# A convolution block: the product steps of a streamed job in one run, row chunks and convolution tile behind them

## The chip, the core and the metric

The kernel runs on one core of a Trainium2 chip. The metric is the device time of one execution in microseconds. The kernel before takes 1061.26 us, the median of 3 runs (1061.01 to 1061.35).

TensorE (PE in the rows) multiplies; VectorE (DVE), ScalarE (ACT) and GpSimdE (POOL) do the rest; SyncE (SP) issues most transfers from memory. Each engine takes its instructions in the order in which they stand in its own queue, and waits at one whose inputs or buffer aren't ready.

## The reference

One layer of a decoder, 256 tokens by 2048 features, in float32. `c` is a condition vector:

```python
mod = silu(c) @ mod_w + mod_b                      # 2048 -> 12288
sh1, sc1, g1, sh2, sc2, g2 = split(mod, 6)
h = rms_norm(x, norm1_g) * (1 + sc1) + sh1
a, gt = split(h @ w_in + b_in, 2)                  # 2048 -> 4096
u = a * sigmoid(gt)
u = depthwise_causal_conv(u, dw_w, 31 taps) + dw_b
y = silu(layer_norm(u, ln_g, ln_b)) @ w_out + b_out
x = x + (1 + g1) * y
h = rms_norm(x, norm2_g) * (1 + sc2) + sh2
x = x + (1 + g2) * (square(relu(h @ w1)) @ w2)     # 2048 -> 8192 -> 2048
```

## The kernel before, in words

Activations lie with features on the 128 partitions and tokens along the row. float32 products run as three products of rounded high parts and remainders: ScalarE writes the high part of a weight half (`hi`, line 245), GpSimdE subtracts it and writes the remainder (`lo`, line 252), and in `mm` two matmuls a step, `hi` by the pair of activations (line 276) and `lo` by the high activations (line 277), give all three.

The product with `w_in` makes 32 column tiles of 128. They go in pairs, one of `a` and one of `gt`: a pair is a job, ("in", 0) to ("in", 15). The first eight jobs share one pass while the input is normalised. The jobs 8 to 15 are streamed: each takes two weight tiles of 1 MB, and its 32 steps (16 for each of the two tiles) are 64 matmuls. Jobs 8 to 14 end in `evac` and `gate`: ScalarE copies one half of the sums (line 953), VectorE adds the other (line 954), ScalarE takes the sigmoid (line 1232) and VectorE multiplies (line 1234, "gate" below). The sums lie in one of two `mm` tiles of PSUM, and these two alternate with the convolution tiles, so that the job after next, or the next one where a convolution lies between, waits for the gate.

Between the jobs other work is handed out by tables. `LATE_IN` gives jobs 8 to 14 row chunks of the modulation matrix, 4, 4, 4, 4, 3, 4 and 1: a chunk is a 1 MB load and four matmuls 32 columns wide that run beside each other (`mod_chunk`, line 737). `CONV_AT` gives the jobs 9, 10, 11, 12, 14 and 15 a convolution tile for TensorE (`pe_conv`, line 1215, 32 matmuls); ScalarE first makes 16 shifted copies (`copy_wide`, line 1189) and afterwards takes the sum out (line 1225). Eight other tiles go over VectorE, tap by tap (lines 1070 to 1076, `advance`). Tile 9 is made by ScalarE's products (line 1129) and GpSimdE's additions (line 1132). `find_shift` (line 1139) sums the first two convolution tiles on TensorE (line 834) and ScalarE makes two copies of the mean (line 1145), which the first taps of the later tiles need (line 1074). After the second group of sixteen chunks a row is copied out (line 744) and folded by four small matmuls (line 781).

Weights and chunks share a ring of five 1 MB buffers (`raw`, line 200). SyncE issues the loads in one fixed order, and a load waits until the buffer's last reader is done: GpSimdE's second `lo` for a weight tile, the four matmuls for a chunk.

A scheduler places the instructions on their engines by its own estimate of when each can run, and `tc.issue_after(x)` says only that an instruction stands behind x. So the queues' order, and not the order of the source, is what the chip sees.

Of the kernel before, what the change touches and what calls it, by code (L numbers as in the profile page):

```python
# [17 lines left out]
KT = D // P  # L18
# [69 lines left out]
def conv_block(ctx: ExitStack, tc: tile.TileContext, x, vec, dwq, c_row, mod_r, mod_c, w_first, w_in, w_out, w1, w2, out):  # L88
# [44 lines left out]
    for i in range(2):  # L133
        p = ps.tile([P, 2, 2 * T], F32, name="mm", bufs=2)
# [6 lines left out]
    state = {"used": 0}  # L141
# [16 lines left out]
    HALF = KT // 2  # L158
# [105 lines left out]
    def mm(p, c, key, acts_of, ks=range(KT), merged=False):  # L264
        halves = parts[key]
        for k in ks:
            hi, lo = halves[k // HALF]
            m = acts_of[k // 2][:, k % 2, :]
            if merged:
                out_p, begin, end = p[:, c, 0:T], k == 0, k == KT - 1  # L270
                w = hi[:, k % HALF, :]
                nc.tensor.matmul(out_p, w, m[:, 0:T], start=begin, stop=False)  # L272
                nc.tensor.matmul(out_p, w, m[:, T : 2 * T], start=False, stop=False)  # L273
                state["mm_end"] = nc.tensor.matmul(out_p, lo[:, k % HALF, :], m[:, 0:T], start=False, stop=end)  # L274
                continue
            nc.tensor.matmul(p[:, c, :], hi[:, k % HALF, :], m, start=(k == 0), stop=(k == KT - 1))  # L276
            state["mm_end"] = nc.tensor.matmul(  # L277
                p[:, c, T : 2 * T], lo[:, k % HALF, :], m[:, 0:T], start=False, stop=(k == KT - 1),
                skip_group_check=True,
            )  # L280
# [446 lines left out]
    def mod_chunk(nb, kg):  # L727
        w = take(("mod", nb, kg))
        group = next(g for g in GROUPS if nb in g)
        b = group.index(nb)  # L730
        begin, end = b == 0 and kg == 0, b == len(group) - 1 and kg == 3
        if begin:
            mod_finish()
            row_ps.append(ps.tile([P, 512], F32, name="row", bufs=1))
        for k in range(4):
            part = w[k // 2][:, 4 * (k % 2) : 4 * (k % 2) + 4, :] if isinstance(w, list) else w[:, 4 * k : 4 * k + 4, :]
            state["row_end"] = nc.tensor.matmul(  # L737
                row_ps[0][32 * k : 32 * k + 32, :], cz[:, 4 * kg + k, 3 - b : 35 - b], part,
                start=begin, stop=end,
            )  # L740
        if end:
            r = tmp.tile([P, 512], F32, name="rowsb", bufs=1)
            with urgent(), tc.issue_after(state["hi_end"]):
                nc.scalar.activation(r, row_ps.pop(), AF.Copy)
            pending.append(([4 * nb for nb in group], 4, r))
# [57 lines left out]
    def mod_col(at):  # L803
        w = take(("col", at)).rearrange("p k n -> p (k n)")
        which, k = divmod(at, KT)
        acc = modc[:, at : at + 1]
        if which == SH2 and "cond" in state:
            n = HALF * P
            for half, total in zip(state["cond"], (acc, rest2[:, k : k + 1])):
                nc.vector.scalar_tensor_tensor(w[:, 0:n], w[:, 0:n], 1.0, half, op0=ALU.mult, op1=ALU.mult, accum_out=total)  # L810
                w = w[:, n:]
            return
        with tc.issue_after(state["e_end"]) if "e_end" in state else ExitStack():
            nc.vector.scalar_tensor_tensor(w, w, 1.0, cb, op0=ALU.mult, op1=ALU.mult, accum_out=acc)  # L814
        if which in amps:
            return nc.vector.scalar_tensor_tensor(
                amps[which][:, k : k + 1], acc, col("modb", at), col("n1g", k), op0=ALU.add, op1=ALU.mult
            )
        elif which != SH2:
            return mod_bias(at, 1, acc)  # L820

    def mods(keys):
        for key in keys:
            if key[0] == "mod":
                mod_chunk(*key[1:])
            else:
                mod_col(key[1])
# [46 lines left out]
    hl = [None] * HALF  # L874
# [86 lines left out]
    p = ps.tile([P, 512], F32, name="small", bufs=1)  # L961
# [10 lines left out]
    with urgent():  # L972
        part = two()[:, 0, :]
        nc.scalar.activation(part, p[:, 0:T], AF.Copy)
        p = ps.tile([P, 512], F32, name="row", bufs=1)
# [8 lines left out]
    for _ in range(2):  # L984
        p = ps.tile([P, 2, 2 * T], F32, name="mm", bufs=2)
# [36 lines left out]
    for k in range(KT):  # L1022
        c = k % 2
# [85 lines left out]
    def advance(n):  # L1109
        for _ in range(n):  # L1110
            next(conv_taps, None)
# [27 lines left out]
    def find_shift():  # L1139
        state["small"] = ps.tile([P, 512], F32, name="small", bufs=1)  # L1140
        p = state["small"][:, 0:T]
        column_sum(p, [cv(k) for k in range(SHIFT)])
        state["shift"] = cp.tile([P, T], F32, name="shift", bufs=1)
        for dst in (state["small"][:, T : 2 * T], state["shift"]):
            nc.scalar.activation(dst, p, AF.Copy, scale=-1.0 / (SHIFT * P))
# [58 lines left out]
    def pe_conv(ct, sq=None, between=None):  # L1204
        wide = wides.pop(ct)
        diag = diags.pop(ct)
        p = ps.tile([P, 2, 2 * T], F32, name="mm", bufs=2)[:, 0, 0:T] if sq is None else ps_two()[:, 0, :]
        if sq is not None:
            nc.tensor.matmul(p, col("ident", 0, P), state["shift"], start=True, stop=False)
        for m in range(8):  # L1210
            if between is not None and m == LAST_TAPS:
                between()
            for g in range(4):
                with tc.issue_after(state["stats_end"].ins) if between is not None else ExitStack():
                    state["conv_end"] = nc.tensor.matmul(  # L1215
                        p[32 * g : 32 * g + 32, :], diag[:, 8 * g + m, :], wide[:, g, 4 * m : 4 * m + T],
                        start=(m == 0 and sq is None), stop=(m == 7),
                    )
        with urgent():
            if ct == 14:  # L1220
                state["cv14"] = nc.vector.scalar_tensor_tensor(
                    cv(ct), p, col("dwb", ct), state["shift"], op0=ALU.add, op1=ALU.add
                ).ins
            elif sq is None:
                nc.scalar.activation(cv(ct), p, AF.Identity, bias=col("dwb", ct))
            else:
                state["cv15"] = nc.vector.tensor_scalar(cv(ct), p, col("dwb", ct), None, op0=ALU.add).ins
                nc.scalar.activation(sq, p, AF.Square, bias=col("dwb", ct))
# [10 lines left out]
    def mix(ct):  # L1239
        pe_conv(ct)  # L1240
        if ct == SHIFT - 1:
            find_shift()
# [16 lines left out]
    for n, job in enumerate(jobs):  # L1259
# [15 lines left out]
        kind, i = job[0], job[-1]  # L1275
        if kind == "out" and i > 0:
            p = ps_two()
        elif not by_tokens(job):
            p = ps.tile([P, 2, 2 * T], F32, name="mm", bufs=2)
# [3 lines left out]
        if job == ("up", 0, 0):  # L1283
            first = mm_shifted(p, 0, job + (0,), False)
            for _ in range(SIDE):
                next(first)
            shift_row(shown.pop(job + (0,)))
            fold_shift()
            for _ in chain(first, mm_shifted(p, 1, job + (1,))):
                pass  # L1290
        elif plain:
            for _ in chain(*[mm_shifted(p, c, job + (c,)) for c in range(2)]):
                pass
        elif job in K_OUTER:
            for k2 in range(HALF):
                for c in range(2):
                    mm(p, c, job + (c,), hl, range(2 * k2, 2 * k2 + 2), True)
        elif kind == "in":
            rows = list(after[job]) if i < KT - 1 else []
            if i == KT - 1:  # L1300
                state["e_end"] = state["copied"]
                mods(cols_in[:COLS_FIRST])
            for c in range(2) if i < KT - 1 else (1, 0):
                for ks in (range(HALF), range(HALF, KT)):
                    mm(p, c, job + (c,), hl, ks, i == KT - 1)
                    with tc.issue_after(state["mm_end"].ins):
                        mods(rows[:1])
                    del rows[:1]
            if i == KT - 1:
                room["hl"] = len(rows_in_hl)  # L1310
                top_up()
        elif by_tokens(job):
            mm_tokens(sums, job)
            state["mm_end"] = state["three_end"]
        else:
            for c in range(2):
                mm(p, c, job + (c,), hl, merged=kind == "out")
        mod_finish()
        if kind == "in":
# [12 lines left out]
            for ct in CONV_AT.get(n, ()):  # L1332
                with tc.issue_after(state["mm_end"].ins):
                    mix(ct)
            advance(ADVANCE.get(n, 0))
            if n in PAIRS_AT:
                pool_pairs(PAIRS_AT[n])
# [34 lines left out]
            rows = after[job][COLS_IN:]  # L1372
# [238 lines left out]
```

## Time and profile before

| | us |
|---|---|
| median of 3 runs | 1061.26 |
| span of the profiled execution, first to last instruction | 1059.2 |
| what lies around the span, median less span | 2.1 |
| first matmul of job 8, in the span | 137.04 |
| first matmul of job 15 | 264.26 |
| TensorE busy | 1042.9 |
| VectorE busy | 918.1 |
| ScalarE busy | 678.2 |
| GpSimdE busy | 280.3 |

All instants below are microseconds from the start of the span. The profile gives the profiled execution's span and no other time of it. A float32 matmul shows as two records, a step's matmuls as one each; records overlap, so the distance from one start to the next tells what a matmul costs, not its own duration.

### The profile page before, as it was taken

The numbers are of one execution on the slowest core, as the hardware profiler recorded it, in microseconds if no ns is written. First come the engines' busy times: TensorE is split into PE (matmuls) and PEld (weight loads), VectorE is DVE, ScalarE is ACT, GpSimd is POOL, SyncE is SP. The second block draws the span as 40 slices with busy tenths as digits, with TensorE's granted clock in tenths as the row PEclk, the third lists the DMA queues.
The fourth block names the chain that finished last, engine by engine and source line by source line (L and its number), as shares of the span: only waits on it lengthen the run. The fifth ranks groups of instructions, "written<-read, shape, count | busy, mean of one in ns | idle before, by whom it ended". The sixth has DMA issues, their size and how long they took to land.

```text
span 1059.2 us, 15571 instructions
## 1 busy us (share of the span) xinstructions
PE 1042.9 (98%) x5712; PEld 853.6 (81%) x5712; DVE 918.1 (87%) x1200; ACT 678.2 (64%) x969; POOL 280.3 (26%) x267
## 2 busy tenths in 40 slices
PE   6999999999999999999999999999999999999998
PEld 3888876676789999877888888888888888888887
DVE  5778779998785889999989999999999999999975
ACT  4111198765776579674777587587687686696771
POOL 0000076979359721001210210111110200113130
PEclk8999999999999999999999999999999999999999
DMA  9999989898989999759998999998999898997892
GB/s 382 420 420 416 411 349 366 308 362 355 368 359 326 357 390 323 215 189 334 332 295 300 279 317 293 274 337 269 279 333 279 280 330 272 282 325 235 308 292 100
DMA packets 75662, 335.20 MB, mean 316 GB/s; under 512 B 9249, under 2 KB 9761, under 8 KB 57409
## 3 DMA queue, kind: packets, MB, share of 16 engines
q1 hardware_dynamic: 57456, 279.53, 70.4%
q0 software_dynamic: 13664, 46.68, 18.1%
q10 hardware_dynamic: 4466, 8.00, 2.0%
q8 instruction: 45, 0.74, 0.3%
q14 instruction: 31, 0.25, 0.1%
HBM read 322.10 MB, written 12.07 MB: 315 GB/s over the span
## 4 chain that ended last, share of the span: by engine, by line
PE 83%; DMA 10%; DVE 4%; ACT 2%; issue 1%; SPq 0%; DVEq 0%; ACTq 0%
PE mm L309 14%; PE mm L308 14%; PE mm L310 14%; DMA raw<-mod_c 7%; PE mm L276 4%; PE acc L309 4%; PE acc L310 4%; PE acc L308 4%; PE acc L272 3%; PE acc L274 3%; PE acc L273 3%; DVE raw L814 2%; PE mm L277 2%; PE row L737 2%; PE mm L1215 1%; PE row L309 1%
## 5 line engine op out<-in xcount | busy, mean ns | idle before, releaser
L324 DVE TENSOR_TENSOR lo<-raw,hi 128x1024 fp32r<-128x1024 f32 x238 | 283.2, 1217 | 30.2 <-ACT hi L327 29.7
L327 ACT ACTIVATE hi<-raw 128x1024 fp32r<-128x1024 f32 x238 | 241.8, 1052 | 71.3 <-DVE raw L324 30.2
L308 PE MATMUL mm<-hi,u 128*128 128x512 f32 x448 | 174.9, 390 | 0.0
L309 PE MATMUL mm<-lo,u 128*128 128x512 f32 x448 | 174.9, 390 | 0.0
L310 PE MATMUL mm<-hi,u 128*128 128x512 f32 x448 | 174.5, 390 | 0.0
L252 POOL TENSOR_TENSOR lo<-raw,hi 128x1024 fp32r<-128x1024 f32 x52 | 124.0, 2410 | 160.5 <-ACT hi L245 160.5
L327 ACT ACTIVATE hi<-s 128x1024 fp32r<-128x1024 f32 x80 | 83.3, 1056 | 101.4 <-DVE s L324 88.9
L814 DVE SCALAR_TENSOR_TENSOR raw<-raw,cond 128x2048 f32<-128x2048 f32 x47 | 109.0, 2323 | 19.4 <-DMA raw<-mod_c 19.4
L324 DVE TENSOR_TENSOR lo<-s,hi 128x1024 fp32r<-128x1024 f32 x80 | 97.5, 1221 | 3.9 <-ACT hi L327 2.3
L309 PEld LDWEIGHTS mm<-lo,u 128*128 128x128 f32 x448 | 84.1, 188 | 18.7 <-DVE lo L324 1.5
L308 PEld LDWEIGHTS mm<-hi,u 128*128 128x128 f32 x448 | 84.2, 188 | 17.8 <-issue 0.2
L310 PEld LDWEIGHTS mm<-hi,u 128*128 128x128 f32 x448 | 84.2, 188 | 17.2
L1076 DVE SCALAR_TENSOR_TENSOR acc<-u,v,acc 128x256 f32<-128x256 f32 x224 | 94.5, 483 | 1.8
L245 ACT ACTIVATE hi<-raw 128x1024 fp32r<-128x1024 f32 x80 | 80.3, 1048 | 11.5 <-DMA raw<-w_in 4.1
L475 POOL DMA_DIRECT2D s<-w x28 | 15.5, 552 | 269.4 <-DVE lo L324 206.6
L276 PE MATMUL mm<-hl,hi 128*128 128x512 f32 x224 | 81.7, 406 | 0.5 <-DVE u L1234 0.5
L1039 ACT ACTIVATE two<-two,modc,amp 128x256 f32<-128x256 f32 x16 | 9.6, 600 | 95.4 <-DVE modc L772 67.6
L999 PE MATMUL mm<-two,first 128*128 128x256 f32 x256 | 60.7, 392 | 7.4 <-ACT two L1039 6.7
L272 PE MATMUL acc<-hl,hi 128*128 128x256 f32 x224 | 63.4, 283 | 0.0
L273 PE MATMUL acc<-hl,hi 128*128 128x256 f32 x224 | 63.4, 283 | 0.0
L277 PE MATMUL mm<-hl,lo 128*128 128x256 f32 x224 | 63.4, 283 | 0.0
L274 PE MATMUL acc<-hl,lo 128*128 128x256 f32 x224 | 63.3, 283 | 0.0
(287 smaller groups left out, 2355.9 us busy)
## 6 DMA issues: line engine op xcount, KB each, us to landing
raw<-w SPq DMA_DIRECT2D x212, 512.0 KB, 6.9
raw<-mod_c SPq DMA_DIRECT2D x56, 1024.0 KB, 11.4
s<-w POOLq DMA_DIRECT2D x68, 512.0 KB, 8.5
raw<-mod_r SPq DMA_DIRECT2D x26, 1024.0 KB, 8.0
raw<-w_in SPq DMA_DIRECT2D x16, 1024.0 KB, 7.0
raw<-w_out SPq DMA_DIRECT2D x16, 1024.0 KB, 9.7
first<-w_first SPq DMA_DIRECT2D x15, 1024.0 KB, 17.2
raw<-mod_c SPq DMA_DIRECT2D x16, 512.0 KB, 12.6
```

The costliest lines, as they stand in the source:

```text
L252: end = by.tensor_tensor(lo, w[:, ks, :], hi.bitcast(F32), op=ALU.subtract)
L272: nc.tensor.matmul(out_p, w, m[:, 0:T], start=begin, stop=False)
L273: nc.tensor.matmul(out_p, w, m[:, T : 2 * T], start=False, stop=False)
L274: state["mm_end"] = nc.tensor.matmul(out_p, lo[:, k % HALF, :], m[:, 0:T], start=False, stop=end)
L276: nc.tensor.matmul(p[:, c, :], hi[:, k % HALF, :], m, start=(k == 0), stop=(k == KT - 1))
L308: nc.tensor.matmul(p, x_hi, w_hi, start=begin, stop=False, skip_group_check=not grouped)
L309: nc.tensor.matmul(p, x_hi, w_lo, start=False, stop=False, skip_group_check=not grouped)
L310: state["three_end"] = nc.tensor.matmul(p, x_lo, w_hi, start=False, stop=end, skip_group_check=not grouped)
L324: ordered("dve", lambda: call(*args, **kw))
L327: ordered("act", lambda: nc.scalar.activation(*args, **kw))
L814: nc.vector.scalar_tensor_tensor(w, w, 1.0, cb, op0=ALU.mult, op1=ALU.mult, accum_out=acc)
L1076: nc.vector.scalar_tensor_tensor(out, s, w, acc, op0=ALU.mult, op1=ALU.add)
```

## The change

The 64 matmuls of a streamed job stand in one run. All row chunks of the job come behind them, then its convolution tile, and the next job's steps behind the last of these.

```diff
-                for ks in (range(HALF), range(HALF, KT)):
-                    mm(p, c, job + (c,), hl, ks, i == KT - 1)
-                    with tc.issue_after(state["mm_end"].ins):
-                        mods(rows[:1])
-                    del rows[:1]
+                with tc.issue_after(state["behind"].ins) if "behind" in state else ExitStack():
+                    mm(p, c, job + (c,), hl, merged=i == KT - 1)
+            with tc.issue_after(state["mm_end"].ins):
+                mods(rows)
+            if rows:
+                state["behind"] = state["row_end"]
...
             for ct in CONV_AT.get(n, ()):
                 with tc.issue_after(state["mm_end"].ins):
                     mix(ct)
+                state["behind"] = state["conv_end"]
```

On TensorE, where job 9 begins, before (`mm_845` holds the sums of job 8, `mm_1017` those of job 9; the `raw` tiles are chunks):

```order
L277 MATMUL mm_845<-hl_653,lo_770 128x256
L276 MATMUL mm_1017<-hl_208,hi_810 128x512
L737 MATMUL row_864<-raw_678,cz_720 32x512 x4
L277 MATMUL mm_1017<-hl_208,lo_811 128x256
L276 MATMUL mm_1017<-hl_208,hi_810 128x512
```

And the same place now:

```order
L277 MATMUL mm_845<-hl_653,lo_770 128x256
L737 MATMUL row_912<-raw_678,cz_720 32x512 x4
L737 MATMUL row_912<-raw_684,cz_720 32x512 x4
L737 MATMUL row_912<-raw_735,cz_720 32x512 x4
L737 MATMUL row_912<-raw_763,cz_720 32x512 x4
L276 MATMUL mm_1017<-hl_208,hi_810 128x512
```

The four chunks of job 8 stood spread over job 9's steps; now all four stand ahead of them.

On TensorE, where the first group's row is folded, before (`mm_1674` is job 12):

```order
L277 MATMUL mm_1674<-hl_388,lo_1437 128x256
L276 MATMUL mm_1674<-hl_450,hi_1440 128x512
L781 MATMUL row_1552<-v_72,rowsb_1550 128x4 x4
L277 MATMUL mm_1674<-hl_450,lo_1441 128x256
L276 MATMUL mm_1674<-hl_450,hi_1440 128x512
```

Now the end of job 11 (`mm_1461`), its chunks, its convolution tile (`mm_1567`) and job 12:

```order
L277 MATMUL mm_1461<-hl_653,lo_1216 128x256
L737 MATMUL row_912<-raw_1301,cz_720 32x512 x4
L737 MATMUL row_912<-raw_1307,cz_720 32x512 x4
L737 MATMUL row_912<-raw_1313,cz_720 32x512 x4
L1215 MATMUL mm_1567<-wide_1219,diag_1422 32x256 x4
L737 MATMUL row_912<-raw_1319,cz_720 32x512 x4
L1215 MATMUL mm_1567<-wide_1219,diag_1422 32x256 x20
L781 MATMUL row_1552<-v_72,rowsb_1550 128x4 x4
L1215 MATMUL mm_1567<-wide_1219,diag_1422 32x256 x8
L276 MATMUL mm_1674<-hl_208,hi_1426 128x512
```

The fold stood three quarters into job 12's steps; now it stands ahead of all of them.

On ScalarE, around the mean that the later taps need (`mm_1331` is the convolution tile behind job 10, `sq` are products for tile 9, `hi` halves of weights), before:

```order
L1129 ACTIVATE sq_1408<-u0_81,v2_79 128x256 x4
L1225 ACTIVATE cv0_716<-mm_1331,v_72 128x256
L1189 ACTIVATE wide_1444<-u1_82 32x284 x16
L1145 ACTIVATE small_1365<-small_1365 128x256
L1129 ACTIVATE sq_1415<-u0_81,v2_79 128x256 x4
L1145 ACTIVATE shift_1368<-small_1365 128x256
L245 ACTIVATE hi_1426<-raw_1199 128x1024
```

And now:

```order
L1129 ACTIVATE sq_1408<-u0_81,v2_79 128x256 x4
L245 ACTIVATE hi_1426<-raw_1199 128x1024
L245 ACTIVATE hi_1430<-raw_1199 128x1024
L1129 ACTIVATE sq_1415<-u0_81,v2_79 128x256 x4
L1225 ACTIVATE cv0_716<-mm_1331,v_72 128x256
L1189 ACTIVATE wide_1444<-u1_82 32x284 x16
L245 ACTIVATE hi_1436<-raw_1209 128x1024
L1145 ACTIVATE small_1365<-small_1365 128x256
L245 ACTIVATE hi_1440<-raw_1209 128x1024
L1145 ACTIVATE shift_1368<-small_1365 128x256
L953 ACTIVATE two_1561<-mm_1461 128x512
```

Two weight halves and the second set of products moved ahead of the convolution's copy, and two more halves ahead of the mean's copies.

## Rows read from the trace of the kernel before

**Rows 1.** The page, busy time of each engine and its share of the span.

```profile
PE 1042.9 (98%) x5712; PEld 853.6 (81%) x5712; DVE 918.1 (87%) x1200; ACT 678.2 (64%) x969; POOL 280.3 (26%) x267
```

**Rows 2.** Timeline of TensorE, job 8: start, duration, line, operation, records, idle before.

```profile
137.04 0.58 PE L276 MATMUL mm<-hl,hi 128*128 128x512 f32 x1
...
148.32 0.39 PE L276 MATMUL mm<-hl,hi 128*128 128x512 f32 x1
148.64 1.07 PE L737 MATMUL row<-raw,cz 128*32 128x512 f32 x8
...
149.86 0.39 PE L276 MATMUL mm<-hl,hi 128*128 128x512 f32 x1
```

**Rows 3.** Timeline of TensorE, chunks in a run, behind job 15.

```profile
290.63 3.62 PE L737 MATMUL row<-hl,cz 128*32 128x512 f32 x32
294.07 1.04 PE L737 MATMUL row<-raw,cz 128*32 128x512 f32 x8
```

**Rows 4.** Line 226 in the stretch of the fourth chunk's load: issue, time to landing.

```profile
L226 SPq DMA_DIRECT2D raw<-mod_r x1: 328/328/328, 149.8 to 149.8; - x1
...
DMA to landing us min/median/max: 5.1/5.1/5.1
```

**Rows 5.** Timeline of VectorE, gates, taps and sums.

```profile
160.39 0.49 DVE L1234 SCALAR_TENSOR_TENSOR u<-mm,v,two 128x256 f32<-128x256 f32 x1 [1.00 <-ACT two L1232]
...
172.34 12.62 DVE L1076 SCALAR_TENSOR_TENSOR acc<-u,v,acc 128x256 f32<-128x256 f32 x32
185.19 0.70 DVE L954 TENSOR_TENSOR mm<-mm,two 128x512 f32<-128x512 f32 x1 [0.24 <-ACT two L953]
...
186.98 0.48 DVE L1234 SCALAR_TENSOR_TENSOR u<-mm,v,two 128x256 f32<-128x256 f32 x1
...
198.88 0.88 DVE L1074 SCALAR_TENSOR_TENSOR acc<-u,v,small 128x256 f32<-128x256 f32 x2 [0.86 <-ACT shift L1145]
```

**Rows 6.** Timeline of ScalarE, halves, sums, sigmoids, copies and products.

```profile
180.11 3.89 ACT L245 ACTIVATE hi<-raw 128x1024 fp32r<-128x1024 f32 x4
...
185.93 0.47 ACT L1232 ACTIVATE two<-mm,v 128x256 f32<-128x256 f32 x1 [0.77 <-DVE mm L954]
...
189.04 0.47 ACT L1225 ACTIVATE cv<-mm,v 128x256 f32<-128x256 f32 x1 [1.05 <-PE mm L1215]
189.41 7.17 ACT L1189 ACTIVATE wide<-u 32x284 f32<-32x284 f32 x16
196.50 0.36 ACT L1145 ACTIVATE small<-small 128x256 f32<-128x256 f32 x1
196.88 1.71 ACT L1129 ACTIVATE sq<-u,v 128x256 f32<-128x256 f32 x4
...
218.03 0.58 ACT L744 ACTIVATE rowsb<-row 128x512 f32<-128x512 f32 x1
```

**Rows 7.** Timeline of GpSimdE, remainders of two weight tiles, a diagonal, sums of products.

```profile
182.18 9.44 POOL L252 TENSOR_TENSOR lo<-raw,hi 128x1024 fp32r<-128x1024 f32 x4
191.57 1.92 POOL L1197 TENSOR_TENSOR diag<-v,dwq_sb 128x1024 f32<-128x1024 f32 x1
193.45 2.65 POOL L1132 TENSOR_TENSOR pairs<-pairs,sq 128x512 f32<-128x512 f32 x2
```

**Rows 8.** Timeline of TensorE, the fold, and from job 14's convolution to job 15.

```profile
221.27 0.95 PE L781 MATMUL row<-v,rowsb 128*128 128x4 f32 x8
...
259.42 3.64 PE L1215 MATMUL mm<-wide,diag 128*32 128x256 f32 x64
262.87 0.39 PE L1155 MATMUL small<-cv,ones 128*32 128x256 f32 x2
...
264.26 0.39 PE L272 MATMUL mm<-hl,hi 128*128 128x256 f32 x1
```

**Rows 9.** Busy time by stretch near the start: stretch, length, engines, TensorE's granted clock.

```profile
20.00:25.00 5.00, 4.72 (x12) 3.81 (x13) 4.66 (x7) 0.88 (x3) 0.00 (x0) 0.53 1.01 421
```

**Rows 10.** Timeline of TensorE, two sets of 16 first products.

```profile
20.28 5.88 PE L999 MATMUL mm<-two,first 128*128 128x256 f32 x16 [4.64 <-ACT two L1039]
...
93.86 3.72 PE L999 MATMUL mm<-two,first 128*128 128x256 f32 x16 [0.88 <-ACT two L1039]
```

## The prediction

> **What bounds the kernel now.** I read the busy shares first: TensorE is busy for 98% of the span, VectorE for 87%, ScalarE for 64%, GpSimdE for 26% [rows 1]. What delays TensorE is therefore paid, unless it idles later anyway; what delays another engine is paid only where TensorE ends up waiting for it. Next I read the streamed stretch on TensorE's timeline. Job 8 begins at 137.04 and job 15 at 264.26, so 127.2 us hold jobs 8 to 14 with 24 chunks and five convolution tiles. Job 8's 64 matmuls take from 137.04 to 148.32, 11.3 us, .176 each and .353 a pair [rows 2]. TensorE hardly waits in this stretch; the releasers that come closest are VectorE's gate, which is followed by the next use of the same PSUM tile, and ScalarE's copies [rows 5, 6].
>
> **The switch that the change removes.** A chunk's four matmuls are 32 columns wide, a step's 128. From one step to the next across one chunk it takes 149.86 − 148.32 = 1.54 us; without the pair itself, .353, the chunk costs 1.19 [rows 2]. In a run of chunks four of them take 294.07 − 290.63 = 3.44, .86 each [rows 3]. So going over to narrow matmuls and back costs .33 for each place, not for each chunk. Of the 24 chunks 16 stand alone among steps now; the other 8 already stand beside a convolution tile, which is narrow too. Afterwards only jobs 8 and 13 have a block of chunks without a convolution tile, so two new places are paid: 14 × .33 = 4.6 us saved. If nothing else moved, job 15 would begin at 259.6.
>
> **The chunk that isn't there yet.** The ring has five buffers, and job 8's fourth chunk goes into that of its first. Before, that load was issued at 149.8, right behind the first chunk, and landed 5.1 later, 154.9, in time for its place three quarters into job 9 [rows 4]. Now it is still issued about 149.8 (the first chunk ends there), but TensorE reaches the fourth chunk at 148.64 + 3 × .86 = 151.2. It waits 154.9 − 151.2 = 3.7 us, and all of job 9 stands behind it. That alone eats four fifths of the saving. It need not reach the end, because VectorE has a later date for job 10 in any case:
>
> **VectorE's order.** In the new order 31 taps and 2 joins stand between job 8's gate and job 9's sum; before there were 16 taps. A tap takes 12.62 / 32 = .39 [rows 5], and I price a join like one. Gate 8 ends near 160.9 (160.39 + .49); 33 × .39 = 12.9 puts job 9's sum at 173.8; from sum to end of gate it is 187.46 − 185.19 = 2.27 in the rows of another job [rows 5], so gate 9 ends at 176.0. Job 10 needs its PSUM tile. TensorE itself, with the 3.7 us, would come at about 174.9 (154.9 + .86 for the chunk, 11.3 for job 9, 3.44 for its chunks, 3.45 for its convolution tile and three switches). So from here the date is VectorE's, whether the chunk was late or not; job 10 runs 176.0 to 187.3, and with four chunks (3.44), a convolution (3.45, below) and two switches job 11 begins near 195.
>
> **ScalarE's order, first place.** The convolution's sum behind job 10 has to be copied out before `find_shift` can use it, a quarter into job 11: there TensorE stands 25 matmuls into the job, 195.1 + 25 × .176 = 199.5. Ahead of this copy on ScalarE stand now two halves (.97 each, 3.89 / 4) and four products (1.71 for four) more [rows 6]. Forward from gate 9: products 1.7, halves 1.95, products 1.7, copy .47, 14 wide copies at 7.17 / 16 = .45 each, 6.3, then two halves and two wide copies, 2.9: 191.0. GpSimdE's last remainder of that tile (9.44 / 4 = 2.36 each) ends near 193.8, its diagonal (1.92) 195.7, and the sum of products (2.65), which frees the buffer of the next four, 198.4 [rows 7]. Against it VectorE: 41 taps (36 before), 16.0, to 192.0, sum and sigmoid to 193.2, so ScalarE's first four products end at 194.9 and its two halves at 196.9. It then waits for GpSimdE: 198.4 + 1.7 + .47 = 200.6. TensorE waits about 1.1 there.
>
> **ScalarE's order, second place.** Behind the copy come 16 wide copies (7.2), a half, the first copy of the mean (.36), a half, the second copy (.36): 200.6 + 7.2 + 2 × (.97 + .36) = 210.5. Before, the second copy came right behind four products [rows 6], and VectorE's first late tap waited .86 for it [rows 5]. Now VectorE is through what stands ahead at about 198.6 and idles 12 us. Then 9 taps (3.5), sum and sigmoid (1.2), four products (1.7), and only then the row's copy (.58 [rows 6]): 217.5. This last is read by the fold, which stood inside job 12's steps and stands now ahead of them, 8 convolution matmuls before. TensorE comes there at 200.6 + .25 + 6.9 (39 matmuls) + .33 + 2.58 (three chunks) + .43 + .86 + 2.16 (24 convolution matmuls and a chunk) = 214.2 and waits 3.3 us.
>
> **The rest, and the sum.** A convolution tile takes 262.87 − 259.42 = 3.45, with what stands behind it ahead of job 15 264.26 − 259.42 = 4.84; the fold .95 [rows 8]. From 217.5: fold .95, 8 convolution matmuls .86, jobs 12 to 14 33.9, their 3, 4 and 1 chunks 6.9, the tiles behind jobs 12 and 14 3.45 + 4.84, three switches 1.0, in all 51.9. Job 15 begins at 269.4, against 264.26: +5.1. I looked for waits that could come behind 217.5: gate 12 near 236 with TensorE due at 237, gate 14 near 268.5 with job 15 due at 269.5; both are just covered. Loads and GpSimdE's remainders have 1.2 to 3 us in hand there by the same reckoning. From job 15 to the end TensorE has hardly a gap (16 us idle in the whole span, 1059.2 − 1042.9 [rows 1]), and the order there does not change, so I carry the 5.1 one to one. The profiled execution's span is 1059.2, 2.1 under the median shown; 1059.2 + 5.1 + 2.1 = **1066.4 us**.
>
> What isn't in the trace of before is TensorE's wait at 214 and what it does to the clock. Lower bound: the estimates of the ScalarE and VectorE chains hold 30 to 40 durations each, and if they come out 3.3 us shorter, the wait is nothing. Upper bound: the wait is 3.3 and the clock falls behind it (third rival). I take the wait without a fall, since the rows with a short wait show none.
>
> **Rivals.** *Only the switches count.* TensorE is busy 98% [rows 1] and a part of the chains gives way: the fourth chunk lands earlier (its buffer comes free sooner) and VectorE isn't late. Then 1061.3 − 4.6 = 1056.7. For it speaks that the .33 is sure; against it, that the load cannot be issued before 149.8 [rows 4] and that 33 VectorE instructions take 12.9 us. It decides from the point where fourth chunk and gate 9 together cost less than 4.6. Chance .07.
>
> *The waits are paid, but only in part.* The fourth chunk's 3.7 alone gives −4.6 + 3.7, 1060.4; the chains without the fold's 3.3 give +1.8, 1063.1. For it speaks that VectorE's 12 us of idling are the end of a long reckoning. Chance .20 together.
>
> *The clock falls in a new wait.* In the stretch 20 to 25 TensorE's granted clock is .53, towards the lower level of 1.2 GHz [rows 9], behind a wait of 4.64, and 16 matmuls took 5.88; behind a wait of .88 the same 16 took 3.72 [rows 10]. The fall costs 2.2. After the fold's 3.3 us, which lies between the two waits, that is 1068.6; after the fourth chunk's wait it would be hidden by gate 9. Chance .23. The Trainium skill, TensorE: Matmul & The Clock Gate, section "Loop structure matters more than you think", says that a long wait for a transfer ahead of the matmuls lets TensorE go cold; by this rule the change, which puts one late chunk ahead of a whole job, brings about just that; the kernel's start shows it for 4.64 us, no row for 3.3.
>
> *Worse.* VectorE's 12 idle us stay with it until job 15's layer norm: 1070 or more. Chance .05.
>
> **How the numbers follow.** My forecast, 1066.4, with its own range 1064.5 to 1067.8, has the remaining .45. Runs of before lie within .03% of each other, and I take .2%, 2.1 us, as about what a measurement of this kernel can tell from no change: 1059.1 to 1063.4. Faster: .07 of the first rival and a little of the 1060.4, .08. Same: the second rival less that, .17 with a bit from the forecast's low side. Slower: forecast, clock and worse, .75. The range 1060.4 to 1069.4 leaves out the first rival, the worst case and the ends.
>
> **What the profile after would show.** Right: the job's 64 matmuls without a narrow one between; a wait of 3 to 4 us at job 8's fourth chunk, ended by its load; gate 9 ending near 176; VectorE idle about 12 us up to 210, ended by the second copy of the mean; TensorE waiting at the fold until about 217; job 15 at 269. Wrong: job 15 ahead of 264, no wait at the fold, VectorE's late tap starting before 205. A granted clock near half behind the fold's wait would show the third rival. If job 15 begins at 269 and the end comes less than 4 us later than before, the step "one to one to the end" failed.

## Result and profile after

The changed kernel takes 1068.43 us, the median of 5 runs (1066.61 to 1068.82), against 1061.26 before: the ratio is 1.0065 (95% interval 1.0053 to 1.0077), 7.2 us slower. Four of the five runs lie between 1068.26 and 1068.82, one at 1066.61; the profiled execution is that one, with a span of 1064.8. What tells a profile of the one level from a profile of the other stands below, in the experiment that runs the kernel once more.

The busy times hardly change: the same work is done [rows 1].

```profile
PE 1042.8 (98%) x5712; PEld 856.8 (80%) x5712; DVE 915.8 (86%) x1200; ACT 677.9 (64%) x969; POOL 280.7 (26%) x267
```

TensorE's timeline of the changed kernel, first the blocks of chunks (start, duration, line, operation, records; in brackets the idle time before and what ended it), then its waits up to job 15:

```profile
148.50 2.78 PE L737 MATMUL row<-raw,cz 128*32 128x512 f32 x24
154.66 1.94 PE L737 MATMUL row<-raw,cz 128*32 128x512 f32 x8 [3.38 <-DMA raw<-mod_r]
156.53 0.80 PE L276 MATMUL mm<-hl,hi 128*128 128x512 f32 x1
...
176.15 0.47 PE L276 MATMUL mm<-hl,hi 128*128 128x512 f32 x1 [0.59 <-DVE u L1234]
...
200.35 0.70 PE L834 MATMUL small<-cv,ones 128*128 128x256 f32 x2 [0.51 <-ACT cv L1225]
...
216.87 1.06 PE L781 MATMUL row<-v,rowsb 128*128 128x4 f32 x8 [2.83 <-ACT rowsb L744]
...
231.72 2.78 PE L737 MATMUL row<-raw,cz 128*32 128x512 f32 x24
...
248.74 0.40 PE L276 MATMUL mm<-hl,hi 128*128 128x512 f32 x1
...
249.18 3.64 PE L737 MATMUL row<-raw,cz 128*32 128x512 f32 x32
252.75 0.50 PE L276 MATMUL mm<-hl,hi 128*128 128x512 f32 x1
...
269.78 0.38 PE L272 MATMUL mm<-hl,hi 128*128 128x256 f32 x1
```

Before, one wait stood in this stretch:

```profile
169.45 0.47 PE L276 MATMUL mm<-hl,hi 128*128 128x512 f32 x1 [0.47 <-DVE u L1234]
```

Now there are four, 7.3 us in all: for the fourth chunk's load, for gate 9, for the convolution's copy, and for the row's copy ahead of the fold. The saving is there as well: from 248.74 to 252.75 it takes 4.01 us, less a pair (.35) 3.66 for four chunks in a block; four that stand alone cost 4 × 1.19 = 4.76 [rows 2]. Job 15 begins 5.5 us later than before (264.26 [rows 8]), and the span is 5.6 us longer: in this execution, what happens up to job 15 is carried one to one.

VectorE in the same kernel, gates 8 and 9 and the late taps (against [rows 5]):

```profile
160.45 0.48 DVE L1234 SCALAR_TENSOR_TENSOR u<-mm,v,two 128x256 f32<-128x256 f32 x1 [1.00 <-ACT two L1232]
...
173.76 0.69 DVE L954 TENSOR_TENSOR mm<-mm,two 128x512 f32<-128x512 f32 x1
...
175.53 0.48 DVE L1234 SCALAR_TENSOR_TENSOR u<-mm,v,two 128x256 f32<-128x256 f32 x1
...
210.02 0.88 DVE L1074 SCALAR_TENSOR_TENSOR acc<-u,v,small 128x256 f32<-128x256 f32 x2 [12.26 <-ACT shift L1145]
```

And ScalarE, the chain that ends in the row's copy (against [rows 6]):

```profile
198.23 1.71 ACT L1129 ACTIVATE sq<-u,v 128x256 f32<-128x256 f32 x4 [1.56 <-POOL pairs L1132]
199.85 0.45 ACT L1225 ACTIVATE cv<-mm,v 128x256 f32<-128x256 f32 x1
200.21 7.18 ACT L1189 ACTIVATE wide<-u 32x284 f32<-32x284 f32 x16
...
209.62 0.36 ACT L1145 ACTIVATE shift<-small 128x256 f32<-128x256 f32 x1
...
216.24 0.58 ACT L744 ACTIVATE rowsb<-row 128x512 f32<-128x512 f32 x1
```

Read together: gate 9 ends 176.0; the copy behind job 10 is late because GpSimdE frees the products' buffer only at 198.2; sixteen wide copies stand between it and the mean; VectorE idles 12.3 us until the mean is there; the sum of job 11, its sigmoid and four products follow; then comes the row's copy, and the fold has waited 2.8 us.

### The profile page after: what moved, and what is told of

The parts are those of the page before. It is cut to its first block, busy times and chain, and to the rows that moved or that the text cites. A ratio compares the mean times of both kernels' runs of the same rounds, so it can differ in the third digit from the quotient of the medians.

```text
span 1064.8 us, 15574 instructions
## 1 busy us (share of the span) xinstructions
PE 1042.8 (98%) x5712; PEld 856.8 (80%) x5712; DVE 915.8 (86%) x1200; ACT 677.9 (64%) x969; POOL 280.7 (26%) x267
## 4 chain that ended last, share of the span: by engine, by line
PE 77%; DMA 11%; DVE 6%; ACT 4%; issue 1%; SPq 0%; POOL 0%; POOLq 0%; ACTq 0%; DVEq 0%
PE mm L309 14%; PE mm L310 14%; PE mm L308 14%; DMA raw<-mod_c 9%; PE acc L310 4%; PE acc L309 4%; PE acc L308 4%; DVE acc L1076 3%; PE acc L274 3%; PE acc L273 3%; PE acc L272 3%; PE mm L276 2%; ACT wide L1189 2%; DVE raw L814 2%; PE row L309 1%; PE row L310 1%
## 5 line engine op out<-in xcount | busy, mean ns | idle before, releaser
L999 PEld LDWEIGHTS mm<-two,first 128*128 128x128 f32 x256 | 49.9, 198 | 17.6 <-ACT two L1039 10.6
```

The source lines that it names most:

```text
L999: step = nc.tensor.matmul(held[n][:, c, :], w[:, 2 * n + c, :], h, start=k == 0 and c == 0, stop=k == KT - 1, skip_group_check=True)
```

## Experiments

All are compared with runs of the kernel before on the same chip (medians 1061.23 to 1061.26).

**The changed kernel once more** (no edit).

> The changed kernel once more. Theory: job 15 begins about 5.5 us later than before in every run; runs that take some 2 us more differ by a stretch at TensorE's lower clock behind one of the new waits (at job 8's fourth chunk, at the fold), so the median comes out between 1066.5 and 1068.9 with the same two levels. Rival: the second level lies in the start, ahead of job 8, and has nothing to do with the change; then a profile of such a run shows job 8 beginning 2 us later than 137.1.

Measured: 1068.72 (1066.59 to 1068.85); four runs at 1068.6 to 1068.9, one at 1066.6. This time the profiled execution is one of the four (span 1066.8). TensorE in it, from the fold to job 12's end, and job 15:

```profile
217.08 1.87 PE L781 MATMUL row<-v,rowsb 128*128 128x4 f32 x8 [2.96 <-ACT rowsb L744]
218.88 1.94 PE L1215 MATMUL mm<-wide,diag 128*32 128x256 f32 x16
220.75 0.80 PE L276 MATMUL mm<-hl,hi 128*128 128x512 f32 x1
...
233.33 2.78 PE L737 MATMUL row<-raw,cz 128*32 128x512 f32 x24
...
271.79 0.39 PE L272 MATMUL mm<-hl,hi 128*128 128x256 f32 x1
```

The busy times by stretch of this run (the third column from the right is TensorE's granted clock):

```profile
216.00:220.00 4.00, 2.92 (x20) 2.38 (x24) 4.00 (x12) 2.59 (x5) 2.86 (x3) 0.60 1.01 426
220.00:224.00 4.00, 4.00 (x19) 2.83 (x12) 3.72 (x11) 2.40 (x6) 4.00 (x2) 0.55 1.01 428
```

and of the profile shown first:

```profile
216.00:220.00 4.00, 3.13 (x29) 2.39 (x30) 4.00 (x11) 2.48 (x4) 2.74 (x3) 0.91 0.99 420
220.00:224.00 4.00, 4.00 (x17) 3.44 (x17) 3.62 (x11) 2.92 (x7) 4.00 (x2) 0.66 1.01 428
```

In both, the clock falls to half, the lower level of 1.2 GHz, behind the fold's wait. In the run shown here it falls at the wait's end (.50 in every microsecond from 217 to 223), so that the fold and the eight convolution matmuls run at it too; in the other it falls some 2 us later (1.00 up to 219, .50 from 220 to 222). From the fold's start to the end of job 12's steps it takes 233.33 − 217.08 = 16.25 in the one, 231.72 − 216.87 = 14.85 in the other. That is 1.4 of the 2.0 us by which job 15 differs; .2 more is the fold's later start. The rest, .4, lies behind job 12, where pairs took .353 in this run and .347 in the other, at a granted clock of 1.00 in both. The fold begins within .2 in the two, and job 8 begins at 136.81 in this run and at 137.12 in the other, so the rival, a start 2 us late, is out. This is read from one profile of each level. The mean clock recorded with each execution does not sort the levels: in the first five it is .997 at 1066.61 and .992 in the others, in these five .992 at 1066.59 and .995 to .997 in the others. That the other executions differ by the same thing is therefore not shown.

**Unread matmuls in the fold's wait.** Twelve matmuls ahead of the fold, which is issued behind them:

```diff
+            if ct == 2 and m == 5:
+                for j in range(12):
+                    with tc.issue_after(state["conv_end"].ins):
+                        state["filler"] = nc.tensor.matmul(whole[:, 1, :], ...)
...
+                if n == 11:
+                    with tc.issue_after(state["filler"].ins):
+                        mod_finish()
```

> As the changed kernel, but TensorE makes 12 matmuls that nothing reads (128x512, 0.23 us each, 2.8 us) ahead of the fold, where it only waited; the fold may move by some tenths. Theory (what the usual run has above 1066.6, and 1.5 us in the better one, is the lower clock behind the fold's wait): the granted clock from 216 to 224 is 1.00, job 12's 64 matmuls take 11.3 us instead of 12.9 to 14.9, and the time is 1064.5 to 1065.5 in nearly all runs, though TensorE has more to do. Rival (the clock falls for another reason, or the two levels have nothing to do with this place): the median stays at 1068 or above.

Measured: 1069.40 (1069.34 to 1069.58). TensorE's timeline of it:

```profile
213.89 3.01 PE L1223 MATMUL mm<-hl,hi 128*128 128x512 f32 x12
216.88 1.05 PE L781 MATMUL row<-v,rowsb 128*128 128x4 f32 x8
...
230.37 2.78 PE L737 MATMUL row<-raw,cz 128*32 128x512 f32 x24
...
238.01 0.47 PE L276 MATMUL mm<-hl,hi 128*128 128x512 f32 x1 [1.40 <-DVE u L1239]
```

and its stretches:

```profile
216.00:220.00 4.00, 4.00 (x35) 2.78 (x34) 4.00 (x11) 2.48 (x5) 2.77 (x3) 1.00 1.01 424
220.00:224.00 4.00, 4.00 (x25) 3.49 (x24) 4.00 (x15) 3.26 (x6) 3.92 (x3) 1.00 1.02 432
```

The part on the clock is shown: with TensorE busy instead of waiting, the clock stays at 1.00, and from the fold to the end of job 12's steps it takes 230.37 − 216.88 = 13.49 instead of 14.85 or 16.25. The part on the time fell: the time is no shorter. The edit also let the scheduler put eight more taps between gate 11 and job 12's sum (45 instead of 37), gate 12 ended at 237.9 instead of 235.6, job 13 waited 1.40 for it, and job 15 began at 269.87. Two more waits for ScalarE, of .83 and .96, follow behind job 15. So what the clock costs by itself, with all orders kept, is 1.4 to 2.8 us of TensorE's path, read from the three timelines; there is no run in which this alone was given back.

**The mean ahead of the wide copies.**

```diff
...
-            with tc.issue_after(state["sg"].ins) if n == HELD else ExitStack():
+            with tc.issue_after(state["sg"].ins) if n == HELD else tc.issue_after(state["mean"]) if n == 11 else ExitStack():
                 copy_wide(COPY_AT[n])
```

> As the changed kernel, but ScalarE's sixteen wide copies for tile 10 are held behind the two copies of the mean. Theory (ScalarE's order is what delays the fold): the copies of the mean end near 202 instead of 210, VectorE's idle stretch shrinks from 12.3 to about 4 us, the fold's 2.8 us wait shrinks to under 0.5 and no lower clock follows it; job 15 begins about 3 us earlier than in the changed kernel, time 1063 to 1064. Rival (VectorE's late taps don't matter, the fold waits for the order of the row's copy alone): idle stretch shrinks, fold still waits over 2 us, time within 0.5 of the changed kernel.

Measured: 1063.13 (1062.88 to 1063.77). VectorE's late taps:

```profile
202.03 0.88 DVE L1074 SCALAR_TENSOR_TENSOR acc<-u,v,small 128x256 f32<-128x256 f32 x2 [4.22 <-ACT shift L1145]
```

TensorE at the fold and job 15:

```profile
214.32 1.06 PE L781 MATMUL row<-v,rowsb 128*128 128x4 f32 x8
...
266.26 0.39 PE L272 MATMUL mm<-hl,hi 128*128 128x256 f32 x1
```

As the theory had it: the mean is there 8 us earlier, the fold waits for nothing, the clock stays at 1.00 from 212 on, and 5.3 of the 7.2 us are back. With the mean ahead of the wide copies the fold's wait is gone, and with the wait filled (above) or gone the clock does not fall there. ScalarE's order is not the only cause of the wait: the held taps, below, shorten it too.

**The fold behind job 12's steps.**

```diff
-        mod_finish()
+        if job != ("in", 11):
+            mod_finish()
```

> As the changed kernel, but the fold of the first row group stands behind job 12's steps instead of ahead of them. Theory: its wait and the lower clock behind it (2.8 + 1.6 us) go, job 12 begins about 3 us earlier, but VectorE's gate of job 12, near 235.5, then holds job 13 (237.9 in the changed kernel), so about 2.2 us are left: time 1064 to 1064.8. Rival (the fold alone carries the loss): all 4.4 us come back, 1062.2 or less.

Measured: 1066.60 (1066.32 to 1068.10), 2 us above the theory. TensorE's waits from job 10 on, and the stretch behind the first of them:

```profile
175.97 0.47 PE L276 MATMUL mm<-hl,hi 128*128 128x512 f32 x1 [2.19 <-DVE u L1234]
...
215.75 0.47 PE L276 MATMUL mm<-hl,hi 128*128 128x512 f32 x1 [0.56 <-DVE u L1234]
...
232.97 2.78 PE L737 MATMUL row<-raw,cz 128*32 128x512 f32 x24 [2.17 <-issue]
```

```profile
176.00:180.00 4.00, 4.00 (x14) 3.42 (x15) 4.00 (x11) 4.00 (x8) 2.36 (x2) 0.57 1.02 430
```

VectorE there:

```profile
231.91 0.69 DVE L954 TENSOR_TENSOR mm<-mm,two 128x512 f32<-128x512 f32 x1
232.51 0.36 DVE L772 TENSOR_TENSOR modc<-row,v 128x4 f32<-128x4 f32 x4
```

Job 12 does begin 3 us earlier. But the fold writes the one `row` buffer that job 12's chunks begin anew, and VectorE reads it out (line 772) only behind job 12's sum: the chunks wait 2.17 us, until that reading. The wait moved by one job. Behind the wait of 2.19 for gate 9 the clock fell (.57), and job 10 took 12.8 us from its first step to its first chunk instead of 11.5; behind the 2.17 it stayed at 1.00 (232 to 240).

**VectorE's taps held behind their job's sums** (and `ADVANCE` as {7: 24, 8: 17, 9: 42, 10: 44, 11: 34, 12: 36, 13: 34, 14: 99}).

```diff
...
-            advance(ADVANCE.get(n, 0))
+            with tc.issue_after(state["added"]):
+                advance(ADVANCE.get(n, 0))
```

> As the changed kernel, but VectorE's taps of a job are held behind the sums of that job, so that 17 instead of 33 instructions stand between the gate of job 8 and the sum of job 9; the orders of TensorE and ScalarE stay. Theory: gate 9 ends near 170 and job 10 no longer waits for it (0.6 us), but job 9's late start (the fourth chunk, 3.4 us) and then GpSimdE's sums and ScalarE's copies keep the next dates (convolution's copy near 199.8, mean near 210), so the time stays within 1 us of the changed kernel, 1066 to 1068.9. Rival (VectorE's order is what costs): 2 us or more come back, 1064.5 or less.

Measured: 1063.90 (1063.19 to 1068.61); the runs scatter, most between 1063.2 and 1065.0. The rival was right. VectorE's sum and gate of job 9:

```profile
170.22 0.70 DVE L954 TENSOR_TENSOR mm<-mm,two 128x512 f32<-128x512 f32 x1 [5.04 <-ACT two L953]
...
172.00 0.48 DVE L1234 SCALAR_TENSOR_TENSOR u<-mm,v,two 128x256 f32<-128x256 f32 x1
```

ScalarE's copy behind job 10 and the row's copy:

```profile
197.99 0.46 ACT L1225 ACTIVATE cv<-mm,v 128x256 f32<-128x256 f32 x1
...
213.88 0.58 ACT L744 ACTIVATE rowsb<-row 128x512 f32<-128x512 f32 x1
```

Gate 9 ends 3.5 us earlier. TensorE gains nothing from it at job 10: it is late itself, by the fourth chunk's wait (3.20) and by the clock behind it (.50 in 156 to 160; from that chunk to the end of job 9 it takes 15.1 us, in the changed kernel's first profile 13.8). But ScalarE's chain gains: its products can begin at 172.5 instead of 176.0, the copy comes 1.9 us earlier, the row's copy 2.4, and the fold waits only 0.94. Behind that wait the clock stays at 1.00. My expectation had GpSimdE hold this chain at its old dates; GpSimdE's chain itself begins with ScalarE's halves behind gate 9.

**Both edits.**

> Both single edits that each brought the time down: the copies of the mean ahead of the wide copies, and VectorE's taps held behind the sums of their job. Theory (gate 9 and the late fourth chunk end within 1 us of each other, so job 10 cannot begin before 175.5 to 176.5 as long as the chunk is late): job 15 about 266, 1062.5 to 1063.9, nearly nothing below the better single edit. Rival (the edits add up): 1060 or less.

Measured: 1062.32 (1061.37 to 1063.92). Job 15 at 265.61; the one wait over .6 that is left is the fourth chunk's, 3.13. The edits don't add up (−5.3 and −4.5 singly, −6.1 together), as the theory had it, but the time is a little below the range given.

**Three chunks for job 8, five for job 9.**

```diff
-LATE_IN = [0] * 8 + [4, 4, 4, 4, 3, 4, 1, 8]
+LATE_IN = [0] * 8 + [3, 5, 4, 4, 3, 4, 1, 8]
```

> As the changed kernel, but the table gives job 8 three chunks and job 9 five, so that the chunk which waited is loaded and multiplied behind job 9; with TensorE's new order the scheduler also places 18 instead of 33 VectorE instructions ahead of job 9's sum and leaves two chunks and the fold inside later jobs. Theory (late chunk and gate 9 together hold job 10 by 4 us): no wait at 151, job 10 begins near 171.5, the fold waits for nothing, and the saved switches show: job 15 at 261 to 264, time 1058 to 1061. Rival (ScalarE's late mean holds everything behind job 10 whatever comes ahead): job 15 at 266 or later, 1063 or more.

Measured: 1063.01 (1062.31 to 1064.85). The wait at 151 is gone; two others for loads came:

```profile
170.46 1.06 PE L737 MATMUL row<-raw,cz 128*32 128x512 f32 x8 [2.33 <-DMA raw<-mod_r]
194.98 1.25 PE L737 MATMUL row<-raw,cz 128*32 128x512 f32 x8 [3.24 <-DMA raw<-mod_r]
```

Neither side had named them. The theory's time was not reached, and the rival's 1063 was met for another reason than its own.

**All three edits.**

> The three edits together: three and five chunks for the jobs 8 and 9, the copies of the mean ahead of the wide copies, VectorE's taps held behind their job's sums. Theory (with all new waits gone only the saved switches are left, 4.6 us less two chunks that still stand alone): TensorE has no wait over 0.6 us from job 8 to job 15, job 15 begins between 260 and 262, time 1057 to 1059, below the kernel before. Rival (VectorE or ScalarE cannot keep the faster pace and set it): waits at the gates of jobs 12 to 14, time 1060 or more.

Measured: 1061.50 (1061.26 to 1062.29), the kernel before within its uncertainty (ratio 1.0004, 0.9995 to 1.0013). One wait is left on TensorE, and again it is a load:

```profile
171.06 1.66 PE L737 MATMUL row<-raw,cz 128*32 128x512 f32 x8 [2.63 <-DMA raw<-mod_r]
...
264.53 0.39 PE L272 MATMUL mm<-hl,hi 128*128 128x256 f32 x1
```

The granted clock is .89 over 160 to 176, a stretch that holds this wait and the fall behind it. That load is issued at 166.2, when GpSimdE is through a weight tile that held the buffer, and lands 4.8 us later; the block, chunks mixed with a convolution tile from 162.6 on, had come to it at 168.4. The theory's 1057 to 1059 was missed by this wait; the rival's 1060 or more was met, but not by the waits that it named.

**Three chunks in the block, the fourth in the middle of the next job** (jobs 8, 9 and 10, with the edits for the mean and the taps).

```diff
...
+                if kept and c == 0:
+                    with tc.issue_after(state["mm_end"].ins):
+                        mods(kept)
...
+            if n in (8, 9, 10):
+                rows, kept = rows[:3], rows[3:]
...
```

> Jobs 8, 9 and 10 keep three of their four chunks in the block and give the fourth to the middle of the next job, as loads that are released late need it; the copies of the mean stand ahead of the wide copies and VectorE's taps behind their job's sums. Theory (the saved switches are real, and what took them back is waits on loads and on the order of the other engines): no wait over 1 us from job 8 to job 15, 14 less 3 switches saved, 3.6 us; job 15 begins near 261, time 1057 to 1059. Rival (VectorE, ScalarE and the transfers together can't go faster than the kernel before): waits turn up elsewhere, job 15 at 263.5 or later, 1060.5 or more.

Measured: 1062.44 (1061.81 to 1062.62); the rival was right. Job 15 begins at 265.46. There is no long wait now, but five short ones, 3.4 us in all:

```profile
204.75 1.06 PE L737 MATMUL row<-raw,cz 128*32 128x512 f32 x8 [0.46 <-DMA raw<-mod_r]
207.23 1.07 PE L737 MATMUL row<-raw,cz 128*32 128x512 f32 x8 [0.55 <-DMA raw<-mod_r]
210.56 1.06 PE L737 MATMUL row<-raw,cz 128*32 128x512 f32 x8 [0.97 <-DMA raw<-mod_r]
213.58 0.47 PE L276 MATMUL mm<-hl,hi 128*128 128x512 f32 x1 [0.66 <-DVE u L1234]
217.06 1.06 PE L781 MATMUL row<-v,rowsb 128*128 128x4 f32 x8 [0.78 <-ACT rowsb L744]
```

With these taken off, job 8 to job 15 takes 125.0 us against 126.7 before: 1.7 of the 3.6 us that the theory had priced. Where the rest went is not shown.

**The two edits on the kernel before.**

> The kernel before with the same two edits for ScalarE's mean and VectorE's taps, chunks spread as before. Theory: TensorE hardly waited there, so they bring nothing: within 0.6 us of 1061.3. Rival (the edits are a gain of their own, and what the combined kernels show is theirs): 1060 or less.

Measured: 1061.53 (1061.36 to 1061.82), ratio 1.0003 (0.9994 to 1.0012). They are no gain of their own. With them in both kernels 1062.3 stands against 1061.5; the runs of the first scatter from 1061.4 to 1063.9, so whether the .8 is the chunks' doing is not shown.

No version beat the kernel before.

## Why the prediction was right, and where it was not

- **The sign, the way and the dates up to the fold: right.** Forecast and profile after: fourth chunk there at 154.9 and 154.66; gate 9 at 176.0 and 176.0; the copy behind job 10 ended 200.6 and 200.3; mean 210.5 and 210.0; VectorE idle 12 and 12.3; the row's copy 217.5 and 216.8; job 15 at 269.4 and 269.8, in the execution that took 1066.6. That the last date and this execution's time fit so closely is in part luck: the fold began .6 earlier than in the sum, the lower clock behind it cost 1.4 that the sum doesn't hold, and the rest took .4 less.
- **The fourth chunk's wait is covered by gate 9: right, by .59 with a lower clock behind the chunk, by 1.41 where the clock stayed at 1.00 (the mean put ahead).** Where gate 9 came earlier (the held taps) it was the chunk, with the lower clock behind it, that set job 10, and the gain at that point was nothing.
- **"I take the wait without a fall": wrong.** The sum put the clock at nothing for a wait of 3.3, on the ground of rows whose wait was .88. The clock fell behind the fold's wait in both profiles of the changed kernel, for 1.4 us over the time at the full clock in the one and 2.8 in the other, and no longer with the wait filled or gone. The wait itself was 2.83 to 2.96, below the 3.3 of the sum. The median, 1068.43, is thus the third rival's 1068.6, to which I gave .23, and not the forecast's 1066.4, whose own range ended at 1067.8. The Trainium skill, TensorE: Matmul & The Clock Gate, section "Loop structure matters more than you think", has TensorE go cold behind a long wait for a transfer. The trace agrees for the waits of 3.3 to 3.4 at the fourth chunk in both profiles of the changed kernel (clock .66 and .77 in 156 to 160), but not for the 3.19 and 3.09 at the same place with the mean put ahead and with the fold later (1.00). At the fold it was a wait for ScalarE, as was the 4.64 at the kernel's start.
- **Switches, 14 × .33 = 4.6: right in kind.** The block of four behind job 13 saved 1.10, against .99 for three switches. Over the stretch, without waits (7.3) and with 1.4 and some 1.3 for the lower clock behind fold and chunk taken off, job 8 to job 15 takes 132.7 − 10.0 = 122.7; before it was 127.2 − .5 = 126.7. That is 4.0 saved. (The 1.3: from the fourth chunk to the end of job 9 it takes 13.8 us here, 12.5 where the clock stayed at 1.00.) The .6 that lacks is not resolved: a wait is counted from the modelled end of a record, and the two paces of the pairs (.347 and .353, below) move such a stretch by some tenths.
- **Two slips that change nothing:** the .353 a pair is an average of job 8's first step, .53, and 31 pairs of .347; and forecast, clock and worse add up to .73, not .75.
- **The rival of the switches alone** needed the fourth chunk and gate 9 together under 4.6 us. With both put right and the mean too, the time only came back to the kernel before's: loads that had been hidden by spreading the chunks are late in a block. My sum had one such load, the fourth of job 8, and that one waited 3.1 to 3.4 us in all seven profiles with that block. With the table changed the wait moved to other loads (2.33 and 3.24; 2.63 with all edits). It isn't so in every block: the four chunks behind job 13 went without a wait, their loads having been issued from 232.8 to 238.2 for a block at 249.2. What counted here is when the block's buffers came free, and two of the five were held by weight tiles until GpSimdE is through.

## To carry to other kernels

Going over from wide to narrow matmuls and back, .33 us here, is a price per place, and putting work of one kind together does save it; but the same work spread out was also the time in which its buffers came free. Before a block is formed, count the buffers that it needs full at its start and who frees them. And where a scheduler sets the queues, one added order on one engine is a new order on all: read each queue that feeds a wait, and price a new wait of 2 to 3 us on TensorE with a possible fall of the clock behind it (here 1.4 to 2.8 us of matmul time), not by its length alone.

## What the runs showed of the hardware that I had not expected

- How soon the clock falls behind a wait of about 3 us differs between two profiles of one program: at the fold at once (the run of 1068.6) or some 2 us later (that of 1066.6).
- The length of the wait alone does not tell whether it falls. Behind the fourth chunk of job 8 it fell to .50 in 156 to 160 with the held taps (wait 3.20), and not at all with the mean put ahead (3.19) or the fold later (3.09). In that last run it fell behind a wait of 2.19 for gate 9 and not behind one of 2.17 for the row buffer. No run here tells what decides it.
- Pairs of product steps took .347 us in some stretches and .353 in others, at a granted clock of 1.00 in both, and in one program now the one and now the other (job 8: .347 in one profile of the changed kernel, .353 in the other). No run here tells what sets it.
